# Two weight transfers moved ahead of a table's reads, the S5 output products placed inside the gate's columns, and one attention buffer moved from one tile to another

## The chip, the cores and the metric

One core of a Trainium2 chip runs the whole program in one launch. The metric is device time in microseconds (us) of one execution; the number compared is the median over runs. TensorE is called PE in the rows, VectorE DVE, ScalarE ACT, GpSimd POOL and SyncE SP; SP issues nearly all the DMA transfers.

## The reference, cut to what matters

Two layers over 256 tokens of width 1024: an attention layer with three branches (compressed, selected, window), then a diagonal state-space layer (S5), each added to the residual, and a last norm.

```python
h = x
h = h + nsa(rmsnorm(h))         # layer 0: attention
h = h + s5(rmsnorm(h))          # layer 1: state space
return rmsnorm(h, final_norm)

def s5(h):
    u, z = split(h @ w_in, 2)             # 1024 columns each
    y = scan(u) + d * u                   # 64 groups of 16 channels, 64 states
    ga, gb = split(gelu(y) @ w_glu, 2)
    return (ga * sigmoid(gb) * silu(z)) @ w_out

def nsa(h):
    # per head: softmax of scores for selected and window keys, times values,
    # plus the compressed branch; gated, times silu(z), times w_out
```

## The kernel before, in words

The program runs through these stages: the norm of x; the projections of layer 0 (their last ones interleaved with the attention); the attention; the output projection of layer 0; the u columns of layer 1's input projection; the scan and the z columns; the GLU; the last projection and the norm. A table for S5 (tiles `bbn`, `ep`) is built on POOL in the background of the attention.

**The attention** works in 24 units, three for each pair of heads (`u` = 0, 1, 2). A unit has four steps. `scores` multiplies on PE into a PSUM bank `su` (L942, L943), adds the distance bias on DVE (L955) into a tile `pt` of probabilities, takes the exponential on ACT (L959), inverts the sums over POOL and DVE (L964 to L966) and scales on ACT (L968). `transposes` turns the four blocks of `pt` on PE (L973) and DVE copies them into a tile `pT` (L975). `values` multiplies `pT` with the values on PE (L986). The loop writes scores of unit n+1, values of unit n-1 and transposes of unit n; between them stand projections that fill PE and steps of the background table. Outside the sections marked `manual_schedule`, a scheduler sets the order of instructions on each engine, so a change of buffers there can move the whole order. `pt` has two buffers and `pT` three.

**The S5 stage** is written in a `manual_schedule`, so that its order is that of the code on PE, ACT, DVE, POOL and SP. All weights pass through four buffers named `raw`, 512 KB each, loaded by SP in the order of the code (L193). `toep_gen` writes the taps of a Toeplitz table to a DRAM tile `kd` (four transfers, L1183) and reads them back shifted into the tile `tm` (eight transfers, 2,304 KB in all, L1186). Then comes, on PE: the u columns of the second half in four chunks (`u_products`, L1448 to L1450), `x1_again`, which transposes the residual again for z, `v_products` and `v_transposed` (the input of the scan; L1312, L1322), the z columns in four blocks of two halves (`z_products`, L1391; one 512 KB weight tile for each half), and `y_products` (L1419, L1420), which read the scan's result `xf` and the table `tm`. `scan_steps` is DVE work. Then the GLU: each 512 KB of weights is split into a high part on ACT (L207) and a low part on DVE or POOL (L209), and PE multiplies three times (L224 to L226). The final norm's row is loaded into a part of `tm` during the GLU (L1530) and scaled on ACT (L1546).

**What SP waits for.** Each DMA counts on one of eight semaphores, DMAHW0 to DMAHW7, in turn; a transfer that takes a semaphore again waits on SP until the one eight places earlier on it has landed. A weight transfer also waits until its `raw` buffer is free.

Of the kernel before, what the change touches and what calls it, by code (L numbers as in the profile page):

```python
# [8 lines left out]
F32 = mybir.dt.float32  # L9
# [7 lines left out]
P = 128  # L17
# [29 lines left out]
def kernel(  # L47
# [52 lines left out]
    def bank(tag="b1", bufs=None):  # L100
        return phase["pool"].tile([P, 512], F32, tag=tag, name=tag, bufs=bufs or phase["bufs"])
# [824 lines left out]
    class Pair:  # L926
# [6 lines left out]
        def scores(self, u):  # L933
# [10 lines left out]
            if u == 0:  # L944
                for hf in range(2):
                    self.b8[hf] = awp.tile([P, S], F32, tag="b8", name="b8", bufs=4)
                    A.activation(self.b8[hf], dist, AF.Copy, scale=-8.0 * _slope(4 * g + 2 * self.pr + hf))
            pt = awp.tile([P, 4, P], F32, tag="pt", name="pt", bufs=2)
            self.pt[u] = pt
# [20 lines left out]
        def transposes(self, u):  # L970
            tb = bank("tu", 1)
            for i in range(4):
                T.transpose(tb[:, i * P:(i + 1) * P], self.pt[u][:, i], ident)  # L973
            self.pT[u] = awp.tile([P, 4, P], F32, tag="pT", name="pT", bufs=3)
            V.tensor_copy(self.pT[u].rearrange("p a q -> p (a q)"), tb)  # L975
# [342 lines left out]
    def v_transposed(hg):  # L1318
# [4 lines left out]
        for ri in range(2):  # L1323
            for q in range(2):
                for u in range(2):
                    o = vh[hg][64 * u:64 * u + 64, ri, 256 * q:256 * q + 256].rearrange("p (t x) -> p t x", t=2)
                    i_ = vb[64 * ri:64 * ri + 64, q].rearrange("p (t u x) -> p u t x", u=2, x=P)[:, u]
                    if q == 0 or hg:
                        A.activation(o, i_, AF.Copy)
                    else:  # L1330
                        V.tensor_copy(o, i_)
# [9 lines left out]
    def scan_steps(hg):  # L1341
# [18 lines left out]
        V.tensor_tensor(w2_, s_, a, op=ALU.mult)  # L1360
        V.tensor_tensor(b_, c_, b_, op=ALU.mult)
        for hf in range(2):
            src = slice(64 * hf, 64 * hf + 64)
# [17 lines left out]

    def z_products(c2):
        zb = bank().rearrange("p (e s) -> p e s", e=2)

        def steps():
            for k0 in range(0, KT, 4):
                w = load_w(w_in1, k0, 4, D + 256 * c2, 2 * P)
                for i in range(4):
# [19 lines left out]

    def y_products(q2):

        yb = bank()
        for q in range(2):
            qd = 2 * q2 + q
            ybv = yb[:, q * S:(q + 1) * S].rearrange("p (l u c) -> p u l c", l=L, u=2)
            for qp in range(2):
                for j in range(4):
# [3 lines left out]
                    T.matmul(o, ut[:, g], tm[:, j, :, 2 * qd + qp], start=False, stop=True, tile_position=(0, 32 * j))  # L1420
        return yb

# [33 lines left out]
    with tc.manual_schedule(engines={E_.PE, E_.Activation, E_.DVE, E_.Pool, E_.SP}):  # L1456
        uw = [u_weights(0), u_weights(1)]
        next(toep)

        sh_ld["xm"].__exit__(None, None, None)  # L1460
# [4 lines left out]
        x1_again(0)  # L1465
        uw.append(u_weights(2))
        v_products(0)
        u_products(1, uw[1])
        raw3 = load_w(w_in1, 6, 2, 512, 512)
        v_transposed(0)  # L1470
        uw.append(split(raw3))
        for _ in toep:
            pass
        u_products(2, uw[2])
# [4 lines left out]
        u_evac(1)  # L1479
        zb, zg = z_products(0)  # L1480
        next(zg)
# [9 lines left out]
        next(scans[0])  # L1491
        z_scaled(0, zb)
        zb, zg = z_products(1)
        for _ in zg:
            pass
        next(scans[1])
        z_scaled(1, zb)
        yb = [y_products(q2) for q2 in range(2)]
        yt = [y_gelu(q2, yb[q2]) for q2 in range(2)]
        zb, zg = z_products(2)  # L1500
# [7 lines left out]
        zb, zg = z_products(3)  # L1508
        for _ in zg:
            pass  # L1510
        z_scaled(3, zb)
        yb = [y_products(q2) for q2 in range(2, 4)]
        yt = [y_gelu(q2, yb[q2 - 2]) for q2 in range(2, 4)]
        for q2 in range(2, 4):
            y_low(q2, yt[q2 - 2])
    yh, yl = yhl
# [124 lines left out]
```

## Time and profile before

| | us |
|---|---|
| median of three runs | 405.45 (405.36 to 406.39) |
| the profiled execution | 405.65 |
| its span, first to last instruction | 403.6 |
| outside the span | 2.05 |
| PE busy within the span | 355.0 (88%) |
| mean granted TensorE clock | 0.945 of full speed |

Durations below are from the profiled execution, so sums are made against 405.65 us. A PE that shows busy is not PE at its peak, since at half clock the same product takes twice as long. Times in rows count from the start of the span.

### The profile page before, as it was taken

The page shows a single profiled execution, that of the slowest core. Times are in us where ns is not written, and L with a number is a line of the kernel's source. Part 1 is how long each engine was busy: PE and PEld are TensorE (multiplying, and loading weights), DVE is VectorE, ACT ScalarE, POOL GpSimd, SP SyncE. Part 2 cuts the span into 40 slices and gives each one's busy share as a digit, 9 for nine tenths or more (in the row PEclk, how much of TensorE's full clock was granted, in tenths as well). Part 3 has the DMA queues.
Part 4 walks back from the last instruction along what each step waited for, and adds up shares of the span by engine and source line. Part 5 has one row for each costly group of instructions (what it writes and reads, how often), then busy time and mean ns, then how long its engine had stood idle before and what let it go on. Part 6 is the DMA issues. An engine that isn't in the chain of part 4 may idle for free.

```text
span 403.6 us, 6667 instructions
## 1 busy us (share of the span) xinstructions
PE 355.0 (88%) x2457; PEld 290.9 (72%) x2457; DVE 215.1 (53%) x572; ACT 175.2 (43%) x401; POOL 237.3 (59%) x261
## 2 busy tenths in 40 slices
PE   3899599999999998986988898991999999999990
PEld 3688468865878887754755776770888889999880
DVE  5969914424445244433455588859157637742323
ACT  3212421145357449565787274440142354454522
POOL 7009459989987789999733749600000126766850
PEclk9699979999999999995899999997799999999996
DMA  8964415457623424511301330999333646655404
GB/s 262 162 176 105 124 54 149 147 179 256 191 75 102 112 97 132 183 52 53 106 0 55 104 106 2 190 133 211 118 106 106 218 149 205 189 181 169 147 0 104
DMA packets 52800, 52.53 MB, mean 130 GB/s; under 512 B 14376, under 2 KB 45216, under 8 KB 52640
## 3 DMA queue, kind: packets, MB, share of 16 engines
q1 hardware_dynamic: 42320, 50.67, 43.7%
q10 hardware_dynamic: 10448, 1.44, 2.5%
q8 instruction: 19, 0.31, 0.3%
q14 instruction: 13, 0.11, 0.1%
HBM read 50.53 MB, written 1.57 MB: 129 GB/s over the span
## 4 chain that ended last, share of the span: by engine, by line
PE 65%; DVE 12%; DMA 10%; POOL 6%; ACT 3%; issue 3%; SPq 0%; DVEq 0%; ACTq 0%; POOLq 0%
PE b L267 16%; PE b L1391 8%; PE b L280 4%; PE b L226 4%; PE b L224 4%; PE b L225 4%; DMA raw<-in_l_w_in_dram 4%; PE ob L986 3%; PE tu L973 3%; DMA tm<-kd 2%; DVE pw L377 2%; POOL wl L209 2%; PE cm L745 2%; PE b L246 2%; POOL bbn L383 1%
## 5 line engine op out<-in xcount | busy, mean ns | idle before, releaser
L267 PE MATMUL b<-xn,raw 128*128 128x256 f32 (+1 forms) x400 | 94.7, 389 | 4.7 <-DVE kl L795 3.4
L209 POOL TENSOR_TENSOR wl<-raw,wh 128x1024 fp32r<-128x1024 f32 x21 | 51.0, 2427 | 69.3 <-ACT wh L207 69.2
L267 PEld LDWEIGHTS b<-xn,raw 128*128 128x128 f32 (+1 forms) x400 | 74.0, 190 | 18.5 <-issue 4.4
L207 ACT ACTIVATE wh<-raw 128x1024 fp32r<-128x1024 f32 x40 | 42.2, 1058 | 42.7 <-PE b L225 11.3
L209 DVE TENSOR_TENSOR wl<-raw,wh 128x1024 fp32r<-128x1024 f32 x19 | 29.2, 1541 | 26.1 <-ACT wh L207 26.1
L1391 PE MATMUL b<-xf,raw 128*128 128x256 f32 x128 | 31.3, 407 | 8.9 <-DMA raw<-in_l_w_in_dram 8.9
L959 ACT ACTIVATE pt<-pt,nm 128x128 f32<-128x128 f32 (+1 forms) x64 | 28.3, 444 | 24.7 <-DVE nm L955 24.6
L226 PE MATMUL b<-yh,wl 128*128 128x256 f32 x128 | 36.1, 284 | 1.1 <-POOL wl L209 1.1
L225 PE MATMUL b<-yl,wh 128*128 128x256 f32 x128 | 36.1, 283 | 0.0
L224 PE MATMUL b<-yh,wh 128*128 128x256 f32 x128 | 36.1, 284 | 0.0
L1391 PEld LDWEIGHTS b<-xf,raw 128*128 128x128 f32 x128 | 25.9, 205 | 13.6 <-DMA raw<-in_l_w_in_dram 9.3
L975 DVE COPY pT<-tu 128x512 f32<-128x512 f32 x24 | 16.6, 690 | 25.4 <-PE tu L973 24.7
L968 ACT ACTIVATE pt<-pt,su 128x128 f32<-128x128 f32 (+1 forms) x64 | 24.6, 444 | 11.6 <-DVE su L966 11.6
L226 PEld LDWEIGHTS b<-yh,wl 128*128 128x128 f32 x128 | 24.5, 192 | 1.4 <-POOL wl L209 1.3
L224 PEld LDWEIGHTS b<-yh,wh 128*128 128x128 f32 x128 | 24.5, 192 | 0.2 <-ACT yh L1431 0.2
L225 PEld LDWEIGHTS b<-yl,wh 128*128 128x128 f32 x128 | 24.5, 192 | 0.0
L383 POOL TENSOR_TENSOR ep<-c1c,pw 128x1024 f32<-128x1024 f32 x8 | 16.0, 2030 | 10.0 <-ACT c1c L546 5.3
L955 DVE CUSTOM_DVE_ANT_0 pt<-su,b 128x128 f32<-128x128 f32 (+1 forms) x64 | 19.4, 350 | 4.7 <-PE su L943 4.7
L383 POOL TENSOR_TENSOR bbn<-bbn,bbt 128x512 f32<-128x512 f32 x16 | 20.4, 1273 | 0.6
L383 POOL TENSOR_TENSOR bbn<-b1c,h 128x512 f32<-128x512 f32 x16 | 17.8, 1110 | 4.6 <-PE bg L604 4.4
L986 PE MATMUL ob<-pT,vsw 128*64 128x128 f32 x192 | 17.2, 296 | 3.4 <-DVE pT L975 3.4
L986 PEld LDWEIGHTS ob<-pT,vsw 128*64 128x64 f32 x192 | 12.6, 146 | 9.1 <-DVE pT L975 4.8
(326 smaller groups left out, 797.8 us busy)
## 6 DMA issues: line engine op xcount, KB each, us to landing
raw<-in_l_w_in_dram SPq DMA_DIRECT2D x44, 512.0 KB, 3.7
raw<-in_l_w_out_dram SPq DMA_DIRECT2D x16, 512.0 KB, 4.0
raw<-in_l_w_glu_dram SPq DMA_DIRECT2D x16, 512.0 KB, 3.6
raw<-in_l_cmp_k_w_dram SPq DMA_DIRECT2D x4, 512.0 KB, 3.9
raw<-in_l_cmp_v_w_dram SPq DMA_DIRECT2D x4, 512.0 KB, 3.9
xin<-in_x_dram SPq DMA_DIRECT2D x2, 512.0 KB
h<-in_x_dram SPq DMA_DIRECT2D x8, 128.0 KB, 3.1
out_dram<-tm SPq DMA_DIRECT2D x5, 128.0 KB, 2.2
```

Source lines behind the costliest of these rows:

```text
L207: A.activation(hi, raw, AF.Copy)
L209: lo_eng[-1].tensor_tensor(lo, raw, hi.bitcast(F32), op=ALU.subtract)
L224: T.matmul(dst, a, xh[:, k], start=(k == 0 and e == 0), stop=False)
L225: T.matmul(dst, a, xl[:, k], start=False, stop=False)
L226: T.matmul(dst, b, xh[:, k], start=False, stop=(k == KT - 1 and e == len(dsts) - 1))
L267: T.matmul(dst, w[:, i, e * m:(e + 1) * m], xn[:, k], start=(k == 0 and e == 0), stop=(k == KT - 1 and e == len(dsts) - 1))
L383: PL.tensor_tensor(o, a, b_, op=op)
L955: V.tensor_tensor_reduce(o.rearrange("p t k -> p (t k)"), sb[:, i * w + br * nk:i * w + (br + 1) * nk], self.b8[hf][:, S - nk:S], -0.125, ...
L959: A.activation(o, o, AF.Exp, scale=-1.0, bias=self.nm[:, j, hf, br:br + 1], accum_out=self.su[:, j, hf, br:br + 1])
L968: A.activation(o, o, AF.Copy, scale=r)
L986: T.matmul(self.ob[64 * hf:64 * hf + 64, j * P:(j + 1) * P], vsw[:, kt, br, 64 * g:64 * g + 64], p_, start=first, stop=last, tile_position ...
L1391: T.matmul(zb[:, e], w[:, i, e * P:(e + 1) * P], xf1[:, k], start=(k == 0 and e == 0), stop=(k == KT - 1 and e == 1))
```

## The change

It has three parts, and two small edits with them.

In the S5 stage all the weight transfers up to z's first block are issued before the Toeplitz reads: the third and fourth u chunks, as before, and now z's two first halves too. The split of the fourth u chunk stands before `v_transposed`, and there the copies by ACT and DVE are divided by `ri` and no longer by `q`. The scan's last four instructions get a `yield` of their own and come after `z_scaled(0)`.

`y_products` for the first two quarters stand between the two halves of z's second block, those of the last two quarters between the halves of z's fourth block; each pair writes a two-bank PSUM tile.

In the attention `pt` gets three buffers and `pT` two.

```diff
@@ -945,7 +945,7 @@
                 for hf in range(2):
                     self.b8[hf] = awp.tile([P, S], F32, tag="b8", name="b8", bufs=4)
                     A.activation(self.b8[hf], dist, AF.Copy, scale=-8.0 * _slope(4 * g + 2 * self.pr + hf))
-            pt = awp.tile([P, 4, P], F32, tag="pt", name="pt", bufs=2)
+            pt = awp.tile([P, 4, P], F32, tag="pt", name="pt", bufs=3)
             self.pt[u] = pt
             parts = []
             for i, hf in enumerate(heads):
@@ -971,7 +971,7 @@
             tb = bank("tu", 1)
             for i in range(4):
                 T.transpose(tb[:, i * P:(i + 1) * P], self.pt[u][:, i], ident)
-            self.pT[u] = awp.tile([P, 4, P], F32, tag="pT", name="pT", bufs=3)
+            self.pT[u] = awp.tile([P, 4, P], F32, tag="pT", name="pT", bufs=2)
             V.tensor_copy(self.pT[u].rearrange("p a q -> p (a q)"), tb)
 
         def values(self, u, pcT):
@@ -1325,7 +1325,7 @@
                 for u in range(2):
                     o = vh[hg][64 * u:64 * u + 64, ri, 256 * q:256 * q + 256].rearrange("p (t x) -> p t x", t=2)
                     i_ = vb[64 * ri:64 * ri + 64, q].rearrange("p (t u x) -> p u t x", u=2, x=P)[:, u]
-                    if q == 0 or hg:
+                    if ri == 0 or hg:
                         A.activation(o, i_, AF.Copy)
                     else:
                         V.tensor_copy(o, i_)
@@ -1359,6 +1359,7 @@
         V.tensor_tensor(w_, s_, b_, op=ALU.mult)
         V.tensor_tensor(w2_, s_, a, op=ALU.mult)
         V.tensor_tensor(b_, c_, b_, op=ALU.mult)
+        yield
         for hf in range(2):
             src = slice(64 * hf, 64 * hf + 64)
             ts = slice(4 * hg, 4 * hg + 4)
@@ -1379,12 +1380,13 @@
         for i in range(4):
             A.activation(xf1[:, 4 * cc + i], b[:, i], AF.Copy, scale=colsT[:, 4 * cc + i:4 * cc + i + 1])
 
-    def z_products(c2):
+    def z_products(c2, raws=()):
+        raws = list(raws)
         zb = bank().rearrange("p (e s) -> p e s", e=2)
 
         def steps():
             for k0 in range(0, KT, 4):
-                w = load_w(w_in1, k0, 4, D + 256 * c2, 2 * P)
+                w = raws.pop(0) if raws else load_w(w_in1, k0, 4, D + 256 * c2, 2 * P)
                 for i in range(4):
                     k = k0 + i
                     for e in range(2):
@@ -1406,9 +1408,8 @@
 
     yhl = [None, None]
 
-    def y_products(q2):
-
-        yb = bank()
+    def y_products(q2, yb):
+
         for q in range(2):
             qd = 2 * q2 + q
             ybv = yb[:, q * S:(q + 1) * S].rearrange("p (l u c) -> p u l c", l=L, u=2)
@@ -1418,7 +1419,6 @@
                     o = ybv[32 * j:32 * j + 32, qp]
                     T.matmul(o, xf[:, g], ep[:, g], start=True, stop=False, tile_position=(0, 32 * j))
                     T.matmul(o, ut[:, g], tm[:, j, :, 2 * qd + qp], start=False, stop=True, tile_position=(0, 32 * j))
-        return yb
 
     def y_gelu(q2, yb):
 
@@ -1456,6 +1456,10 @@
     with tc.manual_schedule(engines={E_.PE, E_.Activation, E_.DVE, E_.Pool, E_.SP}):
         uw = [u_weights(0), u_weights(1)]
         next(toep)
+        raws = [load_w(w_in1, 2 * c, 2, 512, 512) for c in (2, 3)]
+        raws += [load_w(w_in1, k0, 4, D, 2 * P) for k0 in (0, 4)]
+        for _ in toep:
+            pass
 
         sh_ld["xm"].__exit__(None, None, None)
         w1p = ctx.enter_context(tc.tile_pool(name="w1p", bufs=1, reuse_waits="tile"))
@@ -1463,21 +1467,18 @@
         u_evac(0)
         u_products(0, uw[0])
         x1_again(0)
-        uw.append(u_weights(2))
+        uw.append(split(raws[0]))
         v_products(0)
         u_products(1, uw[1])
-        raw3 = load_w(w_in1, 6, 2, 512, 512)
+        uw.append(split(raws[1]))
         v_transposed(0)
-        uw.append(split(raw3))
-        for _ in toep:
-            pass
         u_products(2, uw[2])
         x1_again(1)
         u_products(3, uw[3])
         scans = [scan_steps(0), scan_steps(1)]
         next(scans[0])
         u_evac(1)
-        zb, zg = z_products(0)
+        zb, zg = z_products(0, raws[2:])
         next(zg)
         v_products(1)
 
@@ -1490,13 +1491,17 @@
         next(scans[0])
         next(scans[0])
         z_scaled(0, zb)
+        next(scans[0])
         zb, zg = z_products(1)
-        for _ in zg:
-            pass
+        next(zg)
+        next(scans[1])
+        yb = bank2()
+        for q2 in range(2):
+            y_products(q2, yb[:, q2])
+        yt = [y_gelu(q2, yb[:, q2]) for q2 in range(2)]
+        next(zg)
         next(scans[1])
         z_scaled(1, zb)
-        yb = [y_products(q2) for q2 in range(2)]
-        yt = [y_gelu(q2, yb[q2]) for q2 in range(2)]
         zb, zg = z_products(2)
         for _ in zg:
             pass
@@ -1506,13 +1511,15 @@
             y_low(q2, yt[q2])
         z_scaled(2, zb)
         zb, zg = z_products(3)
-        for _ in zg:
-            pass
+        next(zg)
+        yb = bank2(psu["pool"])
+        for q2 in range(2):
+            y_products(2 + q2, yb[:, q2])
+        yt = [y_gelu(2 + q2, yb[:, q2]) for q2 in range(2)]
+        next(zg)
+        for q2 in range(2):
+            y_low(2 + q2, yt[q2])
         z_scaled(3, zb)
-        yb = [y_products(q2) for q2 in range(2, 4)]
-        yt = [y_gelu(q2, yb[q2 - 2]) for q2 in range(2, 4)]
-        for q2 in range(2, 4):
-            y_low(q2, yt[q2 - 2])
     yh, yl = yhl
     dump("ut", ut)
     dump("tm", tm)
```

The SP queue from the fourth u chunk on, first before (`raw` is a weight tile, `tm` the Toeplitz table, `kd` its source in DRAM; 128x4x256 is a half of a z block):

```order
L193 DMA raw<-in_l_w_in_dram 128x2x512 [waits DMAHW3_49]
L1186 DMA tm<-kd 16x4x2048 [waits DMAHW4_49,DMAHW6_49,DMAHW1_49,DMAHW7_49,DMAHW0_49,Pool_49]
L1186 DMA tm<-kd 16x4x1024 [waits DMAHW5_49]
L1186 DMA tm<-kd 16x4x1792
L1186 DMA tm<-kd 16x4x768
L1186 DMA tm<-kd 16x4x1536
L1186 DMA tm<-kd 16x4x512
L1186 DMA tm<-kd 16x4x1280 [waits DMAHW2_49]
L1186 DMA tm<-kd 16x4x256 [waits DMAHW3_49]
L193 DMA raw<-in_l_w_in_dram 128x4x256 [waits DMAHW4_49,DVE_49]
L193 DMA raw<-in_l_w_in_dram 128x4x256 [waits DMAHW5_49,DVE_49]
L193 DMA raw<-in_l_w_in_dram 128x4x256 [waits DMAHW6_49,DVE_49]
```

and the same stretch of the queue after the change:

```order
L193 DMA raw<-in_l_w_in_dram 128x2x512 [waits DMAHW3_49]
L193 DMA raw<-in_l_w_in_dram 128x4x256 [waits DMAHW4_49,DVE_49]
L193 DMA raw<-in_l_w_in_dram 128x4x256 [waits DMAHW5_49,DVE_49]
L1186 DMA tm<-kd 16x4x2048 [waits DMAHW6_49,DMAHW1_49,DMAHW7_49,DMAHW0_49,Pool_49]
L1186 DMA tm<-kd 16x4x1024
L1186 DMA tm<-kd 16x4x1792
L1186 DMA tm<-kd 16x4x768
L1186 DMA tm<-kd 16x4x1536 [waits DMAHW2_49]
L1186 DMA tm<-kd 16x4x512 [waits DMAHW3_49]
L1186 DMA tm<-kd 16x4x1280 [waits DMAHW4_49]
L1186 DMA tm<-kd 16x4x256 [waits DMAHW5_49]
L193 DMA raw<-in_l_w_in_dram 128x4x256 [waits DMAHW6_49,DVE_49]
```

Two z transfers stand ahead of the eight reads, and the first transfer behind the reads is now the first half of z's second block.

PE from the first half of z's first block on, before (`b_2638` is the bank of z's first block, `b_2731` of its second, `b_2760` that of y):

```order
L1391 MATMUL b_2638<-xf_2477,raw 128x256 x8
L1312 MATMUL b_2649<-bbT_88,ut 32x128 x8
L1312 MATMUL b_2649<-bbT_1040,ut 32x128 x8
L1312 MATMUL b_2668<-bbT_1040,ut 32x128 x16
L1391 MATMUL b_2638<-xf_2477,raw 128x256 x8
L1322 MATMUL b_2703<-ident,vs 128x128 x8
L1391 MATMUL b_2731<-xf_2477,raw 128x256 x16
L1419 MATMUL b_2760<-ep,bbT_88 32x8x16
L1420 MATMUL b_2760<-tm,ut 32x8x16
```

and after (`b_2642` and `b_2731` are the banks of z, `b_2749` is that of y):

```order
L1393 MATMUL b_2642<-xf_2493,raw 128x256 x8
L1312 MATMUL b_2651<-bbT_88,ut 32x128 x8
L1312 MATMUL b_2651<-bbT_1040,ut 32x128 x8
L1312 MATMUL b_2670<-bbT_1040,ut 32x128 x16
L1393 MATMUL b_2642<-xf_2493,raw 128x256 x8
L1322 MATMUL b_2703<-ident,vs 128x128 x8
L1393 MATMUL b_2731<-xf_2493,raw 128x256 x8
L1420 MATMUL b_2749<-ep,bbT_88 32x8x16
L1421 MATMUL b_2749<-tm,ut 32x8x16
```

The first half of z's second block is followed by the y products, which stood behind both halves; the other half comes behind them.

In the attention the scheduler's order changes on each engine. POOL from the last instruction of the background table (`bbn`) on, before (L964 and L965 are a unit's sums, 128x4 for `u` = 0, 128x2 for the others):

```order
L383 TENSOR_TENSOR bbn<-bbn,bbt 128x512
L1024 TENSOR_TENSOR ozf<-part,ozf 128x256
L906 TENSOR_TENSOR sc<-sc,mx 128x128
L1039 TENSOR_TENSOR ozl<-ozf,ozh 128x256
L964 TENSOR_SCALAR su<-su 128x2
L965 TENSOR_TENSOR su<-su,ginv 128x2
L910 TENSOR_SCALAR sm<-sm 128x8
L912 TENSOR_TENSOR sm<-sm,gate 128x8
L913 TENSOR_TENSOR sc<-sc,sm 128x128
L964 TENSOR_SCALAR su<-su 128x4
L965 TENSOR_TENSOR su<-su,ginv 128x4
L964 TENSOR_SCALAR su<-su 128x2
```

and after:

```order
L383 TENSOR_TENSOR bbn<-bbn,bbt 128x512
L1039 TENSOR_TENSOR ozl<-ozf,ozh 128x256
L910 TENSOR_SCALAR sm<-sm 128x8
L964 TENSOR_SCALAR su<-su 128x4
L965 TENSOR_TENSOR su<-su,ginv 128x4
L912 TENSOR_TENSOR sm<-sm,gate 128x8
L913 TENSOR_TENSOR sc<-sc,sm 128x128
L964 TENSOR_SCALAR su<-su 128x2
L965 TENSOR_TENSOR su<-su,ginv 128x2
L964 TENSOR_SCALAR su<-su 128x2
L965 TENSOR_TENSOR su<-su,ginv 128x2
L1039 TENSOR_TENSOR ozl<-ozf,ozh 128x256
```

From the table's end to the end of the attention seven units' sums stood on POOL before, and six stand there now.

## Rows read from the trace of the kernel before

**Rows 1.** The head of the page.

```profile
span 403.6 us, 6667 instructions
```

**Rows 2.** Chain that ended last, 257 to 295 us: start, us, what.

```profile
257.73 10.09 DMA tm<-kd
...
267.88 14.13 DMA raw<-in_l_w_in_dram
...
282.05 6.41 PE b L1391 x16
288.46 1.88 PE b L1312 x64
290.34 3.65 PE b L1391 x16
293.99 0.87 PE b L1322 x8
```

**Rows 3.** PE in order of time, around the wait: start, us, instruction [idle before].

```profile
272.75 0.39 PE L1450 MATMUL b<-wh,xp 128*128 128x512 f32 x1
282.05 6.41 PE L1391 MATMUL b<-xf,raw 128*128 128x256 f32 x16 [8.91 <-DMA raw<-in_l_w_in_dram]
...
323.13 0.39 PE L224 MATMUL b<-yh,wh 128*128 128x256 f32 x1
```

**Rows 4.** Stretches: us, busy of PE, PEld, DVE, ACT, POOL, granted clock, DMA share, GB/s.

```profile
274.00:278.00 4.00, 0.00 (x0) 0.00 (x0) 3.94 (x5) 0.00 (x0) 0.00 (x0) 0.91 1.01 134
278.00:282.00 4.00, 0.00 (x0) 0.00 (x0) 3.97 (x7) 0.00 (x0) 0.00 (x0) 0.50 1.08 302
282.00:286.00 4.00, 3.95 (x9) 3.20 (x10) 1.96 (x3) 0.00 (x0) 0.00 (x0) 0.50 0.61 216
```

**Rows 5.** DMA issues, last row 272.5 to 272.9 us: xcount, KB, us to landing.

```profile
tm<-kd SPq DMA_DIRECT2D x1, 512.0 KB, 10.1
...
tm<-kd SPq DMA_DIRECT2D x1, 192.0 KB, 16.1
...
raw<-in_l_w_in_dram SPq DMA_DIRECT2D x1, 512.0 KB, 11.8
```

**Rows 6.** The eight reads' issues, and a wait of SP ahead of one.

```profile
L1186 SPq DMA_DIRECT2D tm<-kd x8: 303/423/655, 257.7 to 264.1; - x8
...
SPq L1186 <- DMA raw<-in_l_w_in_dram: 2.8, 1, 2.8
```

**Rows 7.** DVE: the last step of u's second half.

```profile
275.47 1.22 DVE L1302 TENSOR_TENSOR ut<-ut,rcolT 128x1024 f32<-128x1024 f32 x1
```

**Rows 8.** Chain that ended last, in the GLU.

```profile
332.06 1.26 POOL wl L209
```

**Rows 9.** ACT: the final norm's row.

```profile
328.84 1.06 ACT L1546 ACTIVATE tm<-tm 128x1024 f32<-128x1024 f32 x1 [3.52 <-DMA tm<-in_final_norm_dram]
```

**Rows 10.** Stretches of the attention, columns as in group 4.

```profile
147.00:160.00 13.00, 11.63 (x64) 9.85 (x62) 6.28 (x23) 11.33 (x32) 11.21 (x16) 1.00 0.35 122
160.00:181.00 21.00, 19.20 (x136) 14.17 (x134) 8.56 (x31) 12.65 (x37) 20.34 (x23) 1.00 0.40 126
181.00:200.00 19.00, 15.69 (x90) 10.58 (x91) 6.80 (x28) 11.77 (x37) 17.40 (x24) 0.64 0.27 77
200.00:223.00 23.00, 19.64 (x134) 13.30 (x132) 13.00 (x53) 17.26 (x56) 8.61 (x22) 1.00 0.10 30
```

**Rows 11.** PE's waits, 147 to 224 us: total us, times, longest.

```profile
PE ob L986 <- DVE pT L975: 3.4, 5, 0.8
PE su L942 <- DVE nm L955: 3.1, 2, 1.6
```

**Rows 12.** ACT: a one-head unit's exponential and scaling.

```profile
217.90 0.51 ACT L959 ACTIVATE pt<-pt,nm 128x256 f32<-128x256 f32 x1 [1.30 <-DVE nm L955]
...
219.80 0.91 ACT L968 ACTIVATE pt<-pt,su 128x256 f32<-128x256 f32 x2 [0.81 <-DVE su L966]
```

**Rows 13.** POOL's longest wait, 147 to 224 us.

```profile
POOL su L964 <- ACT pt L959: 8.5, 5, 2.8
```

## Prediction

> **What bounds the kernel now.** I read the page first, then the chain that ended last, then PE in order of time where the chain leaves PE, then granted clock and DMA rate by stretches, and last the queue of SP. The span is 403.6 us [rows 1]; 2.05 us of the execution's 405.65 lie outside it. Two places matter for this change.
>
> The first is the S5 stage. The chain runs there from a Toeplitz read, 10.09 us, into a weight transfer, 14.13 us, and only then into z's first product [rows 2]. The reader is to see in PE's own order that its last product of u starts at 272.75 and takes 0.39, and that z's first product starts at 282.05 after an idle time of 8.91, ended by that weight transfer [rows 3]. From 274 to 282 PE does nothing. The granted clock is 0.91 of full speed in the first half of this and 0.50 in the second, that is 1.2 GHz of 2.4, and it is still 0.50 from 282 to 286 [rows 4]. So the first half of z's first block takes 6.41 us where the second half, the same 16 records, takes 3.65 [rows 2]. The wait costs 8.91, and 2.76 more because PE comes out of it slow.
>
> The second is the attention between 147 and 223 us. PE is busy 66.2 of these 76 us, so 9.8 are idle, and 181 to 200 runs at a mean clock of 0.64. POOL is busy 17.40 to 20.34 us in the stretches up to 200 that are 19 and 21 long, and only 8.61 of 23 after them [rows 10]. Up to 200 the background table on POOL sets the pace; behind it comes a row of units that hand work from PE to DVE to ACT and back.
>
> **The change part by part: S5.** No product is added or taken away from PE there. From the end of the last u product (272.75 + 0.39 = 273.14) to the first GLU product (323.13) lie 49.99 us [rows 3]; without the 8.91 and the 2.76 the work itself is 38.3.
>
> Why was the weight late? It was issued behind the eight Toeplitz reads, which SP issues from 257.7 to 264.1, the last of them after a wait of 2.8 us for the fourth u chunk [rows 6]. The reads land late: the first after 10.1 us, one of 192 KB after 16.1 [rows 5], while the DMA engines are full (share 1.01) at only 134 GB/s; when the weights' turn comes, the rate is 302 GB/s [rows 4]. Now the two z transfers stand ahead of the reads. They need the raw buffers of the first two u chunks and no read. At 302 GB/s the 1,024 KB take 3.5 us, behind the fourth u chunk, which SP had by 264.1: z's weights are there by about 267.6, ahead of 273.14. So the 8.91 goes, and with it, as PE no longer stops there, the 2.76.
>
> What is late next is the weight behind the reads: z's second block, first half. PE now comes to it at 273.14 + 3.65 + 1.88 + 3.65 + 0.87 = 283.2, by the four rows of the chain at full clock [rows 2]. In the trace the first half of the second block was the third weight behind the reads; issued at about 272.7, it landed 11.8 later, at 284.5 [rows 5]. With the change the bytes ahead of it are the same (two u chunks, the reads, two z halves), only in another order, so I let it land at 284.5 again: a wait of 1.3 us. From below this wait is nothing; from above it is what the two z halves would add if they held up the reads at the reads' own rate, 1,024 KB at 134 GB/s = 7.8 instead of 3.5 us, so 5.6. I take 1.3, since the queue moves the same bytes. **S5: 11.67 - 1.3 = 10.4 us less.**
>
> The small parts of this stage I cost at nothing, with what covers each. The second half of u is ready at 275.47 + 1.22 = 276.7 [rows 7], and PE wants it after z's first half, at 276.8: no cover is left here, and each us that DVE is later would show. The scan's last four instructions now wait for z's first block (282.3) and for one more DVE instruction; three such took 1.96 us [rows 4], so five take 3.3 and end at 285.6, and the y products start at 284.5 + 3.65 = 288.1. The Toeplitz reads are gone from the queue by 278, when the rate changes [rows 4], plus 3.5: 281.5, also in time. The earlier split of the fourth u chunk puts ACT behind its landing at 264.1; the old order had the same chunk split later, with PE's transposes of the residual behind the copies either way. If this chunk came later, ACT and DVE, and behind them `x1_again`, would slip by as much, up to 3.5 us if the z transfers cut in before it.
>
> **The GLU.** PE waits there once in the chain, 1.26 us for a low part on POOL [rows 8]; ACT had stood 3.52 us for the final norm's row ahead of that split [rows 9]. The row's transfer needs the last y products done; these now come one z half, 3.65 us, earlier against the GLU's start, and the transfer stands one weight earlier in the queue. Against this the last z half frees its buffer only as the GLU starts. From 1.26 less to 1.26 more; I take half of the gain, **0.6 less**.
>
> **The attention.** No instruction's work changes. A third `pt` buffer lets scores run one unit further ahead; with two `pT` buffers a copy can wait for older products. By the order POOL has six units' sums behind the table's end where it had seven. One one-head unit is 2 x 0.51 + 0.91 = 1.9 us on ACT [rows 12]. The bounds: at most POOL's idle time up to 200 (53 - 48.95 = 4.05) and PE's after it (3.36) go, 7.4 less [rows 10]; for a loss, the five waits of 3.4 in total for a `pT` copy [rows 11] could double. I take one unit, **1.9 less**. The row has PE waiting for copies that are still running (longest 0.8) as often as for scores. The Trainium skill's "Perfetto Trace Analysis" (section Optimization Strategy) holds that a gap that repeats on an engine can mean too few buffers; by that rule the 3.1 us of PE's waits for scores would go as well, and the attention would give 3.1 instead of 1.9. The trace bears it out only for two of the seven waits.
>
> **Sum.** 10.4 + 0.6 + 1.9 = 12.9 us less: 405.65 - 12.9 = 392.7 for an execution like the profiled one. The median lies 0.2 below that execution, so I forecast 392.5.
>
> **The rivals.**
>
> *z's second block waits instead of its first* (chance 0.10). Everything put ahead of the reads delays them and what is behind them. At the upper price the wait is 5.6, long enough that PE may come out at half clock as it did here, 2.76 more: S5 then gives 11.67 - 8.4 = 3.3, and the time is 392.5 + 7.1 = 399.6. For it speaks that the reads fill the DMA engines at a bad rate [rows 4], against it that no byte is added. The Trainium skill's "DMA: Bandwidth & Descriptors" (Queues, rings and completion order) says that on each DMA engine descriptors are consumed in ring order, but that completion is not first in, first out for an issuing engine. The rows agree so far that the weights behind the reads landed after them.
>
> *The attention gives some back* (0.16). Where `pT` waits, DVE's next unit waits behind the copy, and scores behind that; the waits of 3.4 doubled instead of 1.9 gained make 397.8. I let this case run from 396 to 400.
>
> *The attention gains more* (0.10): with the 7.4 us of the bound instead of 1.9, 387.0.
>
> *Slower* (0.04). POOL serves its instructions in order. It waits 8.5 us in five places for ACT's exponentials, once 2.8 [rows 13], and in the new order more of these sums stand ahead of steps of the table. If the table ended later by such waits, the whole attention would. The rest gives 11.0, so it decides from the fourth added wait of 2.8 us on; with five, 14 us, the time is 408.6. Against it: ACT is idle 7.2 us of the 19 before 200 (19 - 11.77) [rows 10] and works further ahead with a third buffer.
>
> *The change does nothing* (0.02): if z's transfers had to wait for the reads after all, through a buffer or a semaphore. The order shows neither: the reads stand behind them and two of the reads wait for them.
>
> **How the numbers follow.** The forecast with its own range, 389 to 396, has 0.58. Ends of the whole range: below, the attention's larger gain, 387; above, most of the two cases with a loss, 398.5. Outside lie about 0.05 below and 0.14 above, the slower case among them. 0.3%, about 1.2 us, is what a measurement of this kernel can tell from no change. Faster by more than this are the forecast, z's second block, and both attention cases: 0.94; within it 0.02; slower 0.04.
>
> **What would show it right or wrong.** PE has no wait over 2 us between the last u product and the GLU, and the clock is full there; z's first half takes 3.65 and not 6.41; the first GLU product comes 38 to 40 us after the last u product instead of 50. The DMA rate of 302 GB/s comes before the slow stretch and not only behind it. The attention ends (the first `su` products of the output projection run without a break) 0 to 4 us earlier. It is wrong if a wait on L1393 for a transfer, or on L1379 for a copy, takes the place of the old one, or if the table on POOL ends later.

## The result, and the profile after

The changed kernel takes 394.67 us (median; 391.95 to 395.81) beside 405.92 for the kernel before (405.36 to 406.65): ratio 0.9712, interval 0.9656 to 0.9768, so 9.4 to 14.0 us less. The forecast was 392.5, in a range of 387 to 398.5. The changed kernel's executions lie 4 us apart; part of the experiments asks why. Medians here and below are over all runs of a kernel; ratios and their intervals leave out the few runs that the record marks as slow.

The profiled execution has a span of 393.5 us and took 395.42, so 10.1 less in the span than before [rows 1]. The head of its page:

```profile
span 393.5 us, 6675 instructions
```

PE in order of time from the last u product on (start, us, instruction, idle before), to be read against [rows 3]:

```profile
272.90 0.39 PE L1450 MATMUL b<-wh,xp 128*128 128x512 f32 x1
273.12 3.61 PE L1393 MATMUL b<-xf,raw 128*128 128x256 f32 x16
276.67 1.95 PE L1312 MATMUL b<-bbT,ut 128*32 128x128 f32 x64
278.55 3.72 PE L1393 MATMUL b<-xf,raw 128*128 128x256 f32 x16
282.11 1.04 PE L1322 MATMUL b<-ident,vs 128*128 128x128 f32 x8
284.77 3.69 PE L1393 MATMUL b<-xf,raw 128*128 128x256 f32 x16 [1.63 <-DMA raw<-in_l_w_in_dram]
...
313.18 0.47 PE L224 MATMUL b<-yh,wh 128*128 128x256 f32 x1
```

The wait of 8.91 us is gone, z's first half takes 3.61 instead of 6.41, and the next half that is behind the reads is waited for, 1.63 us. From the end of the last u product (272.90 + 0.39 = 273.29) to the first GLU product lie 39.89 us instead of 49.99: 10.1 less. The u products end 0.15 later than before, and from the first GLU product to the end of the span it takes 80.3 instead of 80.5. So in this execution the whole difference is the S5 stage's.

The clock and the DMA rate there, in stretches (columns as in [rows 4]):

```profile
258.00:262.00 4.00, 2.84 (x72) 2.45 (x72) 2.11 (x1) 2.33 (x5) 1.18 (x2) 1.00 0.87 284
...
274.00:278.00 4.00, 4.00 (x61) 3.41 (x63) 3.97 (x4) 0.12 (x1) 0.00 (x0) 1.00 1.04 167
278.00:282.00 4.00, 4.00 (x40) 3.42 (x33) 2.48 (x5) 1.07 (x2) 0.00 (x0) 1.00 1.04 167
282.00:286.00 4.00, 2.37 (x16) 1.96 (x15) 3.58 (x6) 2.88 (x8) 0.00 (x0) 1.00 1.10 367
```

The weights pass at 284 GB/s before the reads, and the clock stays at full speed.

The attention did not get shorter here. The same four stretches as [rows 10]:

```profile
147.00:160.00 13.00, 12.41 (x80) 10.55 (x80) 7.51 (x28) 10.45 (x29) 11.32 (x14) 1.00 0.42 122
160.00:181.00 21.00, 18.07 (x101) 12.32 (x100) 5.88 (x22) 8.86 (x24) 18.21 (x19) 0.84 0.33 103
181.00:200.00 19.00, 16.50 (x114) 11.05 (x112) 9.25 (x41) 14.49 (x48) 18.02 (x30) 1.00 0.16 55
200.00:223.00 23.00, 19.98 (x143) 14.34 (x144) 14.10 (x53) 18.48 (x60) 10.88 (x23) 1.00 0.29 86
```

The low clock moved from the third stretch into the second. The waits there, to be read against [rows 11, 13] (total us, times, longest):

```profile
POOL su L964 <- ACT pt L959: 2.8, 2, 1.9
...
PE b L244 <- DVE ozf L841: 2.2, 1, 2.2
PE ob L986 <- DVE pT L975: 2.1, 4, 0.8
...
PE tu L973 <- DVE pT L975: 1.7, 3, 0.9
...
PE su L942 <- DVE nm L955: 0.6, 1, 0.6
```

The third `pt` buffer did what it should: POOL waits 2.8 us for exponentials instead of 8.5, PE 0.6 for scores instead of 3.1. But the new order has a wait of its own, 2.2 us of PE for a step of the projections' output (L841), and behind it the granted clock is low: 0.84 on the mean from 160 to 181.

### The profile page after: what moved, and what is told of

The parts are those of the page before. It is cut to its first block, busy times and chain, and to the rows that moved or that the text cites. A ratio compares the mean times of both kernels' runs of the same rounds, so it can differ in the third digit from the quotient of the medians.

```text
span 393.5 us, 6675 instructions
## 1 busy us (share of the span) xinstructions
PE 354.3 (90%) x2457; PEld 288.9 (73%) x2457; DVE 213.0 (54%) x572; ACT 173.9 (44%) x401; POOL 237.7 (60%) x261
## 4 chain that ended last, share of the span: by engine, by line
PE 64%; DVE 14%; POOL 9%; DMA 5%; issue 3%; ACT 3%; DVEq 0%; ACTq 0%; POOLq 0%
PE b L267 17%; PE b L1393 5%; PE b L280 4%; PE b L226 4%; PE b L225 4%; PE b L224 4%; DMA raw<-in_l_w_in_dram 3%; PE ob L986 3%; POOL bbn L383 3%; POOL wl L209 3%; PE tu L973 2%; DVE pw L377 2%; DVE wl L209 2%; PE cm L745 2%; PE b L246 1%
## 5 line engine op out<-in xcount | busy, mean ns | idle before, releaser
L207 ACT ACTIVATE wh<-raw 128x1024 fp32r<-128x1024 f32 x40 | 42.2, 1057 | 49.9 <-issue 14.4
L1393 PE MATMUL b<-xf,raw 128*128 128x256 f32 x128 | 28.8, 382 | 1.6 <-DMA raw<-in_l_w_in_dram 1.6
L1393 PEld LDWEIGHTS b<-xf,raw 128*128 128x128 f32 x128 | 24.0, 190 | 5.6 <-issue 2.2
L383 POOL TENSOR_TENSOR ep<-ep,et 128x1024 f32<-128x1024 f32 x8 | 18.9, 2357 | 0.4
```

The costliest lines, as they stand in the source:

```text
L207: A.activation(hi, raw, AF.Copy)
L383: PL.tensor_tensor(o, a, b_, op=op)
L1393: T.matmul(zb[:, e], w[:, i, e * P:(e + 1) * P], xf1[:, k], start=(k == 0 and e == 0), stop=(k == KT - 1 and e == 1))
```

## The experiments

**Without the attention part, and the attention part alone.** The first is the changed kernel with the old numbers of buffers, the second the kernel before with the new ones:

```diff
-            pt = awp.tile([P, 4, P], F32, tag="pt", name="pt", bufs=3)
+            pt = awp.tile([P, 4, P], F32, tag="pt", name="pt", bufs=2)
-            self.pT[u] = awp.tile([P, 4, P], F32, tag="pT", name="pT", bufs=2)
+            self.pT[u] = awp.tile([P, 4, P], F32, tag="pT", name="pT", bufs=3)
```

> The S5 part of the change without its attention part (two buffers of pt, three of pT, as before). Theory 1: the whole gain is S5's; the profile of the changed kernel has the last values product at 223.4 us against 222.8 before, so the buffers give nothing. Then this takes 395 +- 1 us, ratio to before 0.973, with the last values product at 222.5 to 223.5 and 39.9 us from the last u product to the first GLU product. Rival a: the buffers give the 1.9 us that were forecast, and the profiled run hides it: 396.5 or more. Rival b: the buffers cost 1 to 2 us: 393 or less.

> The attention part alone on the kernel before (three buffers of pt, two of pT). Theory 1: within 1 us of the kernel before, 405 to 407, with the attention's end within 1 us of 222.8. Rival a: 404 or less. Rival b: 407 or more. Whatever it is, it should be the difference of the changed kernel to the run without the attention part.

Measured: 395.23 us (393.48 to 398.4), ratio 0.9738 (0.9695 to 0.9781), without it; 405.35, ratio 0.9973 (0.9938 to 1.0007), alone. With 405.9 us before, the S5 part (with whatever the GLU gives) brings 10.6 us and the attention part 1.1 (-0.3 to 2.5), together the 11.7 of the whole change. So neither theory 1 (nothing) nor rival a (1.9) is excluded; rival b (a cost) is.

The profile of the first of the two shows something else: PE waits longer for z's second block, and the block's first half is slow.

```profile
286.84 5.41 PE L1393 MATMUL b<-xf,raw 128*128 128x256 f32 x16 [3.67 <-DMA raw<-in_l_w_in_dram]
```

That profile is of the slowest of the six runs, 398.4 us. The two costs are 3.67 + (5.41 - 3.69) = 5.4 us where the changed kernel's profile has 1.6, in the same order of transfers.

**The loads alone.** Only the transfers are moved; `y_products` and the rest of S5 stand as before.

```diff
         next(toep)
+        raws = [load_w(w_in1, 2 * c, 2, 512, 512) for c in (2, 3)]
+        raws += [load_w(w_in1, k0, 4, D, 2 * P) for k0 in (0, 4)]
+        for _ in toep:
+            pass
...
-        zb, zg = z_products(0)
+        zb, zg = z_products(0, raws[2:])
```

> On the kernel before, only the two z transfers (with the third and fourth u chunk) are put ahead of the Toeplitz reads; y stays behind z's blocks, the splits and the scan stay where they were, the attention as before. Theory 1: the wait of 8.91 us and the half-clock cost of 2.76 go, a wait of 1.6 us for z's second block comes: 396 us, 40 us from the last u product to the first GLU product, with the placement of y worth 0 to 1 us. Rival: the placement of y is needed, since with y behind z the scan or z's second half of the second block is waited for: 398 or more.

Measured: 397.4 us, ratio 0.9781 (0.9743 to 0.9819), 8.9 us less; its profile waits 0.80 for z's second block and has 39.39 us from the last u product to the GLU. The move of the transfers carries most of the gain. The 1.7 us between this and the run without the attention part may come from the placement of y or from the small edits beside it (the split, the copies, the scan's last four instructions), which this run leaves out too; the two intervals overlap, so that it is a gain at all is not shown.

**Filler in the wait.** More products on PE, whose results nobody reads, between the last u product and z's first, in the kernel before:

```diff
         u_evac(1)
+        fb = bank()
+        for i in range(36):
+            T.matmul(fb[:, 0:S], xf1[:, i % KT, 0:P], xf1[:, i % KT], start=True, stop=True)
         zb, zg = z_products(0)
```

> On the kernel before, 36 more products of 128x256 on z's input, 0.228 us each, 8.2 us in all, stand on PE between the last u product and z's first, into a PSUM bank that nobody reads. Theory 1: the transfer still ends the wait at 282, but PE comes out of it at full clock: z's first half takes 3.65 instead of 6.41 us, and the time falls by 2.5 to 3, to 403. Rival: the slow half block has another cause than the clock (the transfer of the weights itself, which shares the DMA engines): no change, 405 to 406.5; or the filler runs beyond 282 and costs: over 406.5.

> The filler in the kernel before, half as long (18 products, 36 records of 0.228 us, 8.2 us). The first filler took 15.7 us and ran past the landing. Theory 1: PE stays at full clock and stops for 0.5 to 1.5 us only; z's first half takes 3.65; 2.5 to 2.9 us faster than the kernel before, 403. Rival: the slow half block has another cause: 405 to 407.

Measured: 411.64 us, ratio 1.0133 (1.0095 to 1.0172), for the long filler. I had taken a product for one record; it makes two, so the filler ran 15.71 us and past the landing:

```profile
274.60 15.71 PE L1482 MATMUL b<-xf 128*128 128x256 f32 x72
290.14 3.62 PE L1391 MATMUL b<-xf,raw 128*128 128x256 f32 x16
```

For the clock it is the cleaner test: PE never stops, the granted clock is 1.00 throughout, z's first half takes 3.62 instead of 6.41, and from z's start to the GLU it is 328.43 - 290.14 = 38.29 us instead of 323.13 - 282.05 = 41.08, so 2.79 less. The rival, that the weights' own transfers slow the half block, is not excluded by this run alone, since they are over by 289 here; the changed kernel excludes it, whose half block takes 3.69 from 284.77 with the DMA engines at a share of 1.10 and the clock at 1.00.

The filler half as long gave 403.9 us, ratio 0.9947 (0.9914 to 0.998), 2.2 us less. Its profiled execution is the slowest of the twelve (409.4 us), so only the order of events is read from it: the filler ended 1.85 us before the landing, and that stop was enough for a half block of 5.41.

```profile
274.84 7.93 PE L1482 MATMUL b<-xf 128*128 128x256 f32 x36
284.62 5.41 PE L1391 MATMUL b<-xf,raw 128*128 128x256 f32 x16 [1.85 <-DMA raw<-in_l_w_in_dram]
```

**The changed kernel again, twice, on two other chips.**

> The changed kernel once more on the chip of these runs. Theory 1: its wait for z's second block differs between executions (1.63 us in its profile, 3.67 and 0.80 in two kernels with the same order of transfers), so the profile shows 0.8 to 4 us there; the median 394 to 396, with a spread of 3 us or more. Rival: the wait is fixed at 1.6 for this order and the spread comes from elsewhere.

> The changed kernel a third time, beside the three others on their chip. Theory 1: 0.969 to 0.973 of the kernel before; its profile shows a wait for z's second block of 0.8 to 4 us and half clock for 4 or 8 us behind the stop near 166. Rival: as fast as the runs with the second block amid the reads.

Measured: 394.96 us (391.47 to 396.61), ratio 0.9709 (0.966 to 0.9758), and 394.99 (392.01 to 396.51), ratio 0.9702 (0.9649 to 0.9755). Theory 1 held in both. With the two profiles there are five of this order of transfers (us; the read is the first of the eight; u to GLU is from the last u product's end to the first GLU product):

| profile | read issued, + landing | z's second block issued | PE waits | its first half | u to GLU |
|---|---|---|---|---|---|
| loads alone | 257.98 + 13.0 | 271.00 | 0.80 | full clock | 39.39 |
| changed, again | 256.03 + 12.9 | 268.95 | 1.01 | 3.69 | 39.28 |
| changed | 258.31 + 14.0 | 272.36 | 1.63 | 3.69 | 39.89 |
| changed, third time | 256.00 + 13.7 | 269.80 | 1.98 | 5.38 | 41.94 |
| no attention change | 258.43 + 15.3 | 273.77 | 3.67 | 5.41 | 43.65 |

In each the transfer is issued within 0.1 us of the first read's landing: it takes that read's semaphore again and waits for it on SP. SP's own rows of the changed kernel (start, us, DMAs), and the read among the DMA issues (KB, us to landing):

```profile
258.31 11.21 SPq L1186 DMA_DIRECT2D tm<-kd  x8
272.36 2.04 SPq L193 DMA_DIRECT2D raw<-in_l_w_in_dram  x2
```

```profile
tm<-kd SPq DMA_DIRECT2D x1, 512.0 KB, 14.0
```

After the issue it is 12.4 to 13.2 us in all five until PE starts. (In two of the five, those with 1.98 and 3.67, the chain of waits names the first read before this transfer; in the other three it names a DVE step that ended at the same time. The five issue times follow the read.) The kernel before had the same hold: z's first weight was issued at 267.88, the first read landed at 257.73 + 10.09 = 267.82 [rows 2].

That this hold makes the weight late is not shown, and another row speaks against it. The last of the eight reads in the changed kernel, and then the weight behind it (start of the issue; KB, us to landing):

```profile
269.21 0.30 SPq L1186 DMA_DIRECT2D tm<-kd  x1
```

```profile
tm<-kd SPq DMA_DIRECT2D x1, 64.0 KB, 14.4
```

```profile
raw<-in_l_w_in_dram SPq DMA_DIRECT2D x1, 512.0 KB, 12.3
```

The last read lands at 269.21 + 14.4 = 283.6, the weight at 272.36 + 12.3 = 284.7, and in the four other profiles the weight lands 1.0 to 1.1 us behind the last read too. The DMA engines are full all that time (shares of 1.04 to 1.10 in the stretches from 274 to 286 above). By these rows the weight comes when the reads ahead of it in the queue are done, and the wait is long where the reads take long; an earlier issue behind the same reads was not tried.

**The second block amid the reads.** In the changed kernel, the first half of z's second block is issued between the fourth and the fifth read:

```diff
-        for _ in toep:
-            pass
+        next(toep)
+        next(toep)
...
         uw.append(split(raws[0]))
+        raws.append(load_w(w_in1, 0, 4, D + 256, 2 * P))
+        for _ in toep:
+            pass
         v_products(0)
...
```

(Further down, the calls of `z_products` are given their tiles to match.)

> The changed kernel, with the first half of z's second block issued between the fourth and the fifth Toeplitz read instead of behind all eight. The profile of the changed kernel waits 1.63 us for this half, and the run without the attention part 3.67 with 1.76 more at a lower clock. Theory 1: these waits are the reads' time ahead of it in the queue: no wait over 0.3 us is left on PE between the last u product and the GLU, which lie 38.3 us apart; 1.6 to 3 us faster than the changed kernel on the same chip, and a smaller spread. Rival: the last four reads, 896 KB, now land behind it and y waits for them, or the DMA engines are the limit and the wait moves to the other half: no change or slower.

> The run with the second block amid the reads once more, on another chip. Theory 1: 0.961 to 0.965 of the kernel before, 2 to 4 us faster than the changed kernel (0.971). Rival: its first result was partly luck, 0.967 to 0.971.

Measured: 390.31 us (388.86 to 392.75), ratio 0.9609 (0.9565 to 0.9653), against 0.9709 for the changed kernel on the same chip; and 392.68, ratio 0.9636 (0.9577 to 0.9694), against 0.9702 on the other. Both are faster than the kernel before. Faster than the changed kernel beyond both intervals is only the first; on the second chip the intervals overlap, and so they do for this order with the row's scaling taken out (0.9674, below). With the old buffers the order gives 0.9727, and behind the reads 0.9738 on another chip. So a gain over the changed kernel is likely, and its size open. Five profiles have this order (these two, and three below): from the last u product to the GLU they take 38.59, 38.60 and 38.60, with no wait for a transfer, and 41.22 and 41.61. The 41.22 is that of the first of these runs: theory 1 asked for no wait over 0.3 us, and the rival's wait shows instead:

```profile
279.38 3.69 PE L1393 MATMUL b<-xf,raw 128*128 128x256 f32 x16 [0.63 <-DMA raw<-in_l_w_in_dram]
285.35 0.27 PE L1421 MATMUL b<-tm,ut 128*32 128x128 f32 x1 [1.94 <-DMA raw<-in_l_w_in_dram]
```

The trace puts the second wait down to a weight, but the product reads `tm`, and the last read, issued at 268.2 with 17.0 us to landing, comes at 285.2. In the profile with 41.61 (old buffers) this wait is 0.57, and most of the rest is a stop amid the y products for which the trace names no releaser:

```profile
292.82 0.34 PE L1420 MATMUL b<-ep,bbT 128*32 128x128 f32 x4 [1.95 <-issue]
```

In the first of these runs PE was 2.1 us earlier than in the changed kernel's profile on that chip (last u product at 268.50, there at 270.60), and had to wait for the reads. The mean over five is 39.7 us against 40.8 in the table, 1.1 less; the medians differ by 4.7 and 2.3. Where the rest of these differences comes from the traces do not tell.

**The row's scaling taken out.** As the first of these, without ACT's scaling of the final norm's row; the factor goes onto the reciprocal in the norm:

```diff
-    A.activation(gf, gf, AF.Copy, scale=RSQRT_C)
...
+        yc = smp.tile([P, 1], F32, tag="yc", name="yc")
+        V.tensor_scalar(yc, y, c, None, op0=ALU.mult)
+        y = yc
```

> As the run before it, and ACT no longer scales the final norm's row during the GLU (the factor goes onto the norm's reciprocal, one small DVE instruction for each half of the tokens at the end). Theory 1: ACT's wait for the row is why POOL's low part is late and PE waits 0.9 to 1.0 us in the GLU; without it this wait goes and the end pays 0.1 to 0.3: 0.6 to 0.9 us faster than the run before it. Rival: POOL is late by itself, the wait stays: no change or 0.2 slower.

Measured: 394.74 us, ratio 0.9674 (0.9618 to 0.9731), not faster than its partner. The profile has no wait of PE in the GLU and needs 79.4 us from the first GLU product to the end; but the changed kernel's second profile, with a wait of ACT of 4.6 us for the row, has no such wait either and needs 79.3. The wait for POOL's low part comes and goes without this edit; the theory is not confirmed.

**Old buffers, and two of each, with the second block amid the reads.**

> S5 part, first half of z's second block between the fourth and fifth read, attention as before (two buffers of pt, three of pT). Beside the run with the new attention buffers on the same chip this is the attention part, with S5's varying wait mostly gone. Theory 1: PE stops once near 166 us with the new buffers and runs at half clock for 4 or 8 us behind it, where the old order runs at half clock for 13 us (183 to 196); so the new buffers end the attention at 221.2 or 223.4 and the old ones at 223.0: this is 0 to 2 us slower than its partner, 0.965 of the kernel before. Rival: they are equal or the old buffers faster.

> As the two others, with two buffers of pt and two of pT. Theory 1: it is the third pt buffer that moves the order; with two of each the time is that of the old buffers or 0 to 2 us more, since only pT copies can wait longer. Rival: fewer buffers alone give the order and the stop near 166, and the time of the new buffers.

Measured on one chip: ratio 0.9727 (0.9646 to 0.9808), median 397.32 us, with the old buffers; 0.9763 (0.9713 to 0.9814), 396.75 us, with two of each; 0.9636 (0.9577 to 0.9694), 392.68 us, with the new ones. The old buffers are 3.7 us behind the new ones by the ratios, but these intervals overlap and the two profiles' attentions end within 0.2 us of each other (rows below), so this run decides neither for theory 1 nor for the rival. Two of each is slower than the new buffers beyond both intervals, so with two `pT` buffers the third `pt` buffer is what helps. That the missing `pT` buffer costs shows in the trace alone; the intervals of two of each and of the old numbers overlap. The attention's last products in the three, two of each first, then the old ones, then the new:

```profile
226.49 1.09 PE L986 MATMUL ob<-pT,vsw 128*64 128x128 f32 x14 [0.78 <-DVE pT L975]
```

```profile
222.30 1.09 PE L986 MATMUL ob<-pT,vsw 128*64 128x128 f32 x14 [0.78 <-DVE pT L975]
```

```profile
222.49 1.09 PE L986 MATMUL ob<-pT,vsw 128*64 128x128 f32 x14 [0.42 <-DVE pT L975]
```

With the new buffers that start has two places in seven profiles: 222.5 to 222.6 (three) and 220.2 to 220.6 (four). What differs is the clock behind PE's stop near 166 us: here 168 to 176 in the changed kernel's first and second profile, columns as before:

```profile
164.00:168.00 4.00, 1.46 (x9) 0.79 (x7) 1.53 (x4) 2.29 (x6) 4.00 (x6) 1.00 0.93 307
168.00:172.00 4.00, 3.92 (x14) 2.40 (x16) 0.15 (x1) 0.54 (x2) 3.92 (x5) 0.61 0.21 82
172.00:176.00 4.00, 4.00 (x24) 2.30 (x22) 1.11 (x2) 0.52 (x1) 1.45 (x3) 0.54 0.00 0
```

```profile
168.00:172.00 4.00, 4.00 (x21) 2.28 (x23) 0.23 (x1) 0.00 (x0) 3.84 (x4) 0.62 0.02 9
172.00:176.00 4.00, 4.00 (x39) 2.96 (x35) 1.64 (x4) 1.93 (x4) 3.08 (x3) 1.00 0.01 2
```

In the first the clock is low in both stretches from 168 on, in the second only in one, and the attention ends 2.3 us earlier.

## Why the prediction was right, step by step

*S5, 10.4 forecast.* The mechanism was right: the wait of 8.91 went and the 2.76 of the slow half block with it (2.79 in the filler's trace). The changed kernel's profile gives 10.1, the executions without the attention part 10.6. The wait for z's second block was forecast at 1.3, by a landing at 284.5, and shows 1.63, by one at 284.7. That the size came out so close is partly luck: over the five profiles of this order the wait is 0.80 to 3.67. The reason given, the same bytes ahead of the transfer in the queue, fits the landings 1.0 to 1.1 us behind the last read. What I did not see is that SP holds the transfer until the first read has landed, though the rows of the kernel before show this hold too, and that the reads take a different time in each execution, 12.9 to 15.3 us for the first. The Trainium skill's "DMA: Bandwidth & Descriptors" (Anatomy of one DMA — SWDGE (gpsimd) path) says that DMA engines do not wait on semaphores and that a wait happens on the issuing sequencer before dispatch. The five issue times agree with it for SP's transfers.

The prediction read the reads as gone at 278 before and at 281.5 after, from the DMA rate; the last one landed at 283.6. The y products start at 288.4, so this cost nothing here; with z's half passed between the reads it cost the 1.94 us above.

*The rival "z's second block waits instead"* came true in part: in two of five profiles the wait is 1.98 and 3.67 and PE comes out of it at the lower clock, at a price of 3.7 and 5.4 us instead of the 8.4 priced. It is one of the reasons why the changed kernel's executions differ by some us.

*The attention, 1.9 forecast, 1.1 measured* (-0.3 to 2.5). Of its step "a third buffer lets scores run one unit further ahead" the waits on POOL and PE show that it happens. What I did not see is that the new order stops PE for 2.2 us near 166, ahead of a projection, and that the clock is low behind it for one or two stretches of 4 us; the old order had its low clock between 181 and 196. By the start of the last products (222.0 to 222.5 with the old buffers in four profiles, 223.7 and 223.9 in the two filler runs, whose attention is the old one as well; about 222.5 or 220.4 with the new) the gain is mostly 2 us or nothing, by which of the two it is. The interval of the attention part alone holds both nothing and the 1.9. (The prediction counted PE's waits for copies as often as those for scores; its row has five and two, which speaks more for the copies.) The table on POOL, which by the prediction sets the pace up to 200, in fact ends later, which the prediction had named as a sign of being wrong. Its last instruction, before and after:

```profile
195.90 1.27 POOL L383 TENSOR_TENSOR bbn<-bbn,bbt 128x512 f32<-128x512 f32 x1
```

```profile
200.77 1.28 POOL L383 TENSOR_TENSOR bbn<-bbn,bbt 128x512 f32<-128x512 f32 x1
```

It ends 4.9 us later, and the attention at most 0.6 later for it: behind the table there is less left to do. The rival "slower" named POOL as its place; POOL's waits for exponentials fell to 2.8 instead.

*The GLU, 0.6 forecast.* 0.2 in the profile. ACT waited longer for the norm's row, 5.56 us instead of 3.52 [rows 9], not less, and the chain through POOL's low part cost 1.01 instead of 1.26 [rows 8]; by the run without the scaling and the changed kernel's second profile that wait is not tied to the row alone.

*The sum* was 12.9 us, measured are 11.7, and the interval (9.4 to 14.0) holds both. By the two part runs 0.8 of the difference is the attention's and 0.4 that of S5 and the GLU together (10.6 of 11.0); neither is clear of the noise.

## What to carry to other kernels

Look for the transfer that is late next when one is moved ahead, and see what its landing follows: here the end of the slow reads ahead of it in the queue, in all five profiles. A semaphore held its issue as well; whether such a hold costs anything asks for a run of its own. A slow transfer that comes in pieces can be divided, so that what is wanted first passes between its parts; here that gained on one chip and lay within the noise on another. When one more buffer removes waits, see where PE stops in the new order: a stop of 2 us could bring a slow clock behind it that cost about as much again (1.98 and 1.69 us at z's second block).

## What the runs showed of the hardware that I had not expected

**DVE and POOL can lengthen each other's steps.** In the first run with the second block amid the reads the last u product starts at 268.50, 2.4 us earlier than in the run beside it without the row's scaling (270.89), though the two kernels do not differ there and their attentions end 0.1 us apart. The norm's small steps on DVE run there beside the scan's table on POOL. DVE's two splits and POOL's next steps, in the earlier execution first:

```profile
248.81 3.61 DVE L209 TENSOR_TENSOR wl<-raw,wh 128x1024 fp32r<-128x1024 f32 x2
```

```profile
249.43 3.96 POOL L383 TENSOR_TENSOR tab<-tab 128x512 f32<-128x512 f32 x2
253.36 1.29 POOL L383 TENSOR_TENSOR tab<-tab,tab 128x512 f32<-128x512 f32 x1
```

```profile
250.31 4.38 DVE L209 TENSOR_TENSOR wl<-raw,wh 128x1024 fp32r<-128x1024 f32 x2
```

```profile
249.26 2.12 POOL L383 TENSOR_TENSOR tab<-tab 128x512 f32<-128x512 f32 x2
251.33 2.27 POOL L383 TENSOR_TENSOR tab<-tab,tab 128x512 f32<-128x512 f32 x1
```

In the earlier execution the splits run beside POOL's first two steps, which take 3.96 us, and the third takes 1.29. In the later one these two are half over when the splits start and take 2.12; the third runs beside the splits and takes 2.27. A split takes 1.8 and 2.2 on the mean in these rows; while POOL stands, it takes 1.23 (the earlier execution):

```profile
258.57 1.23 DVE L209 TENSOR_TENSOR wl<-raw,wh 128x1024 fp32r<-128x1024 f32 x1 [2.83 <-ACT wh L207]
```

So steps of both engines are longer in places where the two overlap, and what runs beside what differs between executions. PE waits for DVE here. Of the 2.4 us the splits account for 4.38 - 3.61 = 0.8; another 1.5 is there when they start (248.81 and 250.31). The Trainium skill's "SBUF — State Buffer" (Who interferes with whom) says that a DVE instruction with two inputs in SBUF contends with a GpSimd instruction that reads SBUF, over a port pair that the two engines share. These rows agree with it. That it is this port was not tried.

**Short stops, either clock.** Of the waits for z's second block, 0.80, 1.01 and 1.63 us were followed by a half block at full clock, 1.98 and 3.67 by one of 5.4 us, with a granted clock of 0.50; so was the 1.85 of the half filler. The third execution of the changed kernel, behind its wait of 1.98 (columns as before):

```profile
284.00:286.00 2.00, 2.00 (x6) 1.56 (x5) 1.97 (x5) 1.66 (x2) 0.00 (x0) 0.50 0.58 202
```

The length of the stop alone does not decide: those of 1.94 and 1.95 us at the y products, with the second block amid the reads, left the clock at 1.00.
